# RWKV systems' stage: TensorE's order written in the program, 192 pieces of projection with the systems' steps between them

## The chip, the cores and the metric

The kernel runs on one core of a Trainium2 chip. The metric is the device time of one execution, in microseconds (us). Five engines take part, each with a queue of its own that it works off in order: TensorE (PE, matmuls), VectorE (DVE), ScalarE (ACT), GpSimd (POOL) and SyncE (SP, which issues the DMAs).

## The reference

A two-layer trunk, a gated DeltaNet layer and then an RWKV-7 layer, over 1104 tokens (16 meta tokens and 1024 of a prompt, 8 samples of 8 tokens), 1024 channels. The change is in the RWKV layer. For each of its 16 heads, with a 64x64 state `S`:

```python
rkvz = jnp.einsum('sbtd,sde->sbte', xs[:4], w_rkvz)          # four projections, 1024 x 1024 each
r, k, v, z = rkvz[0], rkvz[1], rkvz[2], rkvz[3]
kk = l2norm((k * k_k).reshape(B, T, H, N))
...
def step(S, inp):
    r_t, k_t, v_t, d_t, kk_t, b_t = inp                      # b = kk * a
    S = (S * d_t[:, :, None, :]
         + jnp.einsum('bhvk,bhk->bhv', S, -kk_t)[..., None] * b_t[:, :, None, :]
         + v_t[..., None] * k_t[:, :, None, :])
    return S, jnp.einsum('bhvk,bhk->bhv', S, r_t)
```

The kernel doesn't step token by token. It cuts time into chunks of 64 tokens; in a chunk the steps are a lower triangular 64x64 system for each head, built from `kk`, `a` and the decays, and the inverse of that system is all that the later walk over the chunks needs.

## The kernel before

The program has three parts: the DeltaNet layer (to about 1300 us), a stage in which the RWKV layer's projections and systems are made (the subject here), and a wave that walks over the chunks and ends with the output projection.

**Projections.** Each of r, v and z (`m` = 0, 2, 3) is 8 output tiles of 128 channels, over three segments of the tokens (384, 384, 336 columns; z has the first two here). One tile and segment is 24 matmuls into one PSUM buffer `d`: 8 slices of the inputs (`xa`, `xc`, `xh`, `xl`), each as high times high, low times high and high times low of a float32 split in two parts (`whi`, `wlo` of the weights). `project` (L1152) loads a tile's weights, runs its segments and has ACT copy (or gate) the result to `ev` and SP store it. Ahead of each `m`, `mix` (L1017) makes the inputs: per slice and segment two instructions on ACT, one or two on DVE into `mixs`, and a low part on DVE or POOL.

**Systems.** There are 24 items (8 pairs of heads, 3 segments), an item has 6 chunks. `rwkv_inverse` (L1293) takes a group of five items, in these steps:

- preparation: loads of the cumulated decays, `a` and `k` (`sldcs`, `slda`, `sldk`); ACT scales `k` to `skk` and takes two exponentials (`sDp`, `siD`) and a square (`sgl`); DVE makes `sal` (L1285) and, after POOL's product with `a` (L1310), the final `skk` (L1311); both are stored for the wave
- the item's system: 12 products of 64x64 on PE into PSUM `fL`, and the sums of squares by one matmul with the two-column mask `hmask` into PSUM `frss`; ACT copies `fL` to `sgl`, DVE copies `frss` to `rkc` (L1327), and SP stores both to DRAM (`rltd`, `rssd`). `fL` and `frss` share two PSUM buffers
- of the group, read back from DRAM: scales (`bblk`, and `rk` by a transpose `fbpp`), then 120 blocks of 32x32 at once in `invA`; DVE scales `invA` (L470) and inverts all blocks by 31 pairs of a product `invtmp` and a subtraction in `invT` (L452, L454). `invT` has one buffer: POOL clears it (L446, L447) once the previous group's inverse is stored
- the merge of each item (`inverse_merge`, L506): 12 products `mY` of 32x32 on PE, scaled by DVE to `invY` (L518), and 12 products `mU` with `sTT`, which ACT negates into `sTT`; POOL scales it (L1336) and SP stores it to DRAM `ttd`. `sTT` has three buffers for the five items of a group, which POOL clears (L484) and DMAs fill from the stored inverse.

**What sets the order.** The program calls `rwkv_inverse` after output tiles 1, 4, 7, 10 and 13 of the 24, with a group's five items and five merges at one place. A scheduler then orders each engine's queue when the program is built, from its own estimates of time: an instruction that it thinks ready may go ahead of others of the program. The order on the chip is fixed from then on. Only the wave's PE order is the program's own (`manual_schedule` in `layer1`).

## Time and profile before

| | us |
|---|---|
| median of three runs | 2360.84 (2356.81 to 2362.48) |
| the profiled execution's own time | 2362.64 |
| its span, first to last instruction | 2360.9 |
| PE busy | 2167.1 (92%) |
| DVE busy | 1571.2 (67%) |
| ACT busy | 1282.6 (54%) |
| POOL busy | 949.4 (40%) |

The stage runs from the first matmul of r at 1460.1 us to the first of the wave's (`zz`) at 1861.0 us of the span. A row of the profile names the line, the engine, the operation, and the tile written and those read; busy time of PE counts matmuls that overlap only once, so a stretch is read by starts. "Idle before" is the idle time of the engine just ahead of an instruction, with what ended it.

### The profile page before, as it was taken

To read this page: it belongs to the slowest core of one execution; us is meant where nothing else is said; L and a number is where in the kernel's file an instruction comes from. 1 tells how busy PE (TensorE), PEld (TensorE's weight loads), DVE (VectorE), ACT (ScalarE), POOL (GpSimd) and SP (SyncE) were. 2 spreads that over 40 slices of the span, in tenths; PEclk is the share of its full clock that TensorE was granted. 3 is DMA by queue.
4 is the path that set the end of the run, shared out by engine and by line. 5 is a ranking of instruction groups with operands and counts; after the bars stand their busy time and mean duration, and the time that the engine had idled before them with its cause. 6 is when DMAs were issued, how large, how long until landed. Compare 5 with 4: busy or idle time off the path is not lost. (4 is left out here: it accounts for less than half of the span.)

```text
span 2360.9 us, 54503 instructions
## 1 busy us (share of the span) xinstructions
PE 2167.1 (92%) x19737; PEld 1961.9 (83%) x19737; DVE 1571.2 (67%) x4219; ACT 1282.6 (54%) x3599; POOL 949.4 (40%) x1318
## 2 busy tenths in 40 slices
PE   6989999999999999999999999999888888899886
PEld 5888989889898989898989998887777866778775
DVE  6878677685858686774345833479878456667754
ACT  5455545564656555456333746646444355677763
POOL 3445333443435353434232523446445423344433
PEclk9999999999999999999999999998999998999998
DMA  3423332323233333335152145577774654677753
GB/s 113 107 76 104 88 94 78 101 75 105 78 101 91 90 102 88 109 90 184 48 163 83 52 163 175 182 199 197 188 181 130 178 160 143 178 220 227 215 153 126
DMA packets 499719, 308.89 MB, mean 131 GB/s; under 512 B 208089, under 2 KB 484826, under 8 KB 499450
## 3 DMA queue, kind: packets, MB, share of 16 engines
q1 hardware_dynamic: 499450, 305.41, 45.6%
q8 instruction: 156, 2.56, 0.5%
q14 instruction: 113, 0.93, 0.1%
HBM read 209.97 MB, written 95.33 MB: 129 GB/s over the span
## 5 line engine op out<-in xcount | busy, mean ns | idle before, releaser
L90 POOL TENSOR_TENSOR wlo<-wraw,whi 128x512 fp32r<-128x512 f32 (+2 forms) x252 | 332.4, 1322 | 359.8 <-ACT whi L86 334.4
L76 PE MATMUL d<-xc,whi 128*128 128x384 f32 (+2 forms) x910 | 260.2, 344 | 8.1 <-ACT whi L86 3.6
L86 ACT CAST whi<-wraw 128x512 fp32r<-128x512 f32 (+2 forms) x252 | 151.7, 603 | 138.8 <-PE dq L76 50.7
L419 DVE SCALAR_TENSOR_TENSOR cvy<-raw,cw,cvy 128x408 f32<-128x408 f32 (+2 forms) x288 | 178.3, 632 | 15.7 <-ACT cvy L62 13.8
L452 DVE TENSOR_TENSOR invtmp<-invA,invT 72x31 f32<-72x31 f32 (+31 forms) x403 | 172.7, 429 | 18.7 <-POOL invT L447 8.0
L76 PEld LDWEIGHTS d<-xc,whi 128*128 128x128 f32 (+1 forms) x910 | 168.9, 193 | 15.2 <-ACT whi L86 4.7
L454 DVE TENSOR_TENSOR invT<-invT,invtmp 72x31 f32<-72x31 f32 (+31 forms) x403 | 172.3, 428 | 6.6
L76 PE MATMUL dz<-xc,whi 128*128 128x384 f32 (+1 forms) x480 | 149.4, 343 | 0.0
L76 PE MATMUL dv<-xc,whi 128*128 128x384 f32 (+1 forms) x480 | 146.8, 335 | 0.0
L76 PE MATMUL d<-xa,whi 128*128 128x384 f32 (+3 forms) x450 | 141.4, 348 | 4.1 <-DVE xa L90 2.8
L76 PE MATMUL d<-xc,wlo 128*128 128x384 f32 (+2 forms) x428 | 143.9, 345 | 0.7 <-POOL wlo L90 0.7
L868 POOL TENSOR_SCALAR Sb<-Sb,eglb 128x128 f32<-128x128 f32 x128 | 80.4, 645 | 87.6 <-DMA Sb<-in_state_gdn 36.6
L76 PE MATMUL dz<-xa,whi 128*128 128x384 f32 (+1 forms) x288 | 100.3, 348 | 0.0
L76 PE MATMUL dv<-xa,whi 128*128 128x384 f32 (+1 forms) x288 | 99.9, 347 | 0.1
L76 PEld LDWEIGHTS d<-xa,whi 128*128 128x128 f32 (+1 forms) x450 | 85.2, 194 | 12.8 <-issue 5.2
L76 PEld LDWEIGHTS dz<-xc,whi 128*128 128x128 f32 x480 | 89.5, 192 | 0.8
L76 PEld LDWEIGHTS dv<-xc,whi 128*128 128x128 f32 x480 | 88.6, 188 | 0.5 <-issue 0.4
L76 PE MATMUL d<-xa,wlo 128*128 128x384 f32 (+3 forms) x252 | 86.6, 344 | 0.0
L62 ACT ACTIVATE o<-rA,gcol 128x128 f32<-128x128 f32 x128 | 46.6, 372 | 72.6 <-DVE S L779 72.0
L76 PE MATMUL d<-xh,wlo 128*128 128x384 f32 (+1 forms) x256 | 83.9, 343 | 2.0 <-POOL wlo L90 2.0
L76 PEld LDWEIGHTS d<-xc,wlo 128*128 128x128 f32 (+1 forms) x428 | 82.1, 194 | 4.0 <-issue 1.9
L76 PE MATMUL d<-xh,whi 128*128 128x384 f32 (+1 forms) x256 | 84.5, 344 | 0.5 <-ACT whi L86 0.5
(509 smaller groups left out, 7012.3 us busy)
## 6 DMA issues: line engine op xcount, KB each, us to landing
wraw<-in_gdn_w_in SPq DMA_DIRECT2D x96, 256.0 KB
wraw<-in_rwkv_w_rkvz SPq DMA_DIRECT2D x80, 256.0 KB
Sb<-in_state_gdn SPq DMA_DIRECT2D x64, 256.0 KB
wraw<-in_rwkv_w_o SPq DMA_DIRECT2D x40, 256.0 KB
E<-drow SPq DMA_DIRECT2D x24, 384.0 KB
attn<-drow SPq DMA_DIRECT2D x24, 384.0 KB
wraw<-in_gdn_w_out SPq DMA_DIRECT2D x36, 256.0 KB
out_s_gdn<-Sb SPq DMA_DIRECT2D x32, 256.0 KB
```

The source lines that it names most:

```text
L62: return self.nc.scalar.activation(out, in_, func, bias=bias, scale=scale, **kw)
L76: self.nc.tensor.matmul(out, lhsT, rhs, start=start, stop=stop)
L86: nc.scalar.copy(hi, x)
L90: e.tensor_tensor(lo, x, hi.bitcast(F32), op=ALU.subtract)
L419: nc.vector.scalar_tensor_tensor(y[:, 0:wd], raw[:, k:k + wd], cw[k], y[:, 0:wd], op0=ALU.mult, op1=ALU.add)
L452: nc.vector.tensor_tensor(tmp, A[:, j, j + 1:32].unsqueeze(2).broadcast_to([nb, n, m]), Tv[:, j, 0:m].unsqueeze(1).broadcast_to([nb, n, m] ...
L454: nc.vector.tensor_tensor(Tv[:, j + 1:32, 0:m], Tv[:, j + 1:32, 0:m], tmp, op=ALU.subtract)
L868: nc.gpsimd.tensor_scalar(Sb[:, u], Sb[:, u], self.eglb[:, hv, 4 * g + u:4 * g + u + 1], None, op0=ALU.mult)
```

## The change

`project` becomes a generator, `project_units`, that stops after each eight matmuls: 16 tiles of nine units and 8 of six, 192 in all. `rwkv_inverse` becomes `inverse_plan`, a table from the number of a unit to the steps that follow it; the whole runs under `manual_schedule` for PE, so that PE's order is the program's. The other engines' queues are still the scheduler's. An item's system (`lower`) stands after unit 9, 12, 15, 18, 21 for the first five items and every four units after that, its preparation (`prepare`) 5 or 7 units earlier. The group's inverse is called two units after its last item. The merge is split into a left half (`mY`, `merge_left`) and a right half (`mU`, `merge_right`), which stand two units apart, three units from item to item, from 35 units after the first group's last item and 27 units after the end of the group before (or later).

Buffers: `sal` and `bk` (before `skk`) are two halves of a tile with two buffers, the squares have a buffer of their own (`ssq`), and `skk` is now `k`'s own load. The loads of decays, `a` and `k` are one DMA (`cak`), `r` and `v` in the wave one (`rv`), the stores of `sal` and `bk` one (`abd`). The mask has 32 columns, and the sums of squares are three matmuls of 128 columns into three quarters of the partitions, copied by DVE as 96x128 and stored by three DMAs. One memset of each item on POOL is gone.

```diff
...
+    def dense_units(self, w, xh, xl, seg):
+        c0, n = SEGS[seg]
+        p = self.ps("d", 4)
+        his, los = w
+        for c in range(24):
+            k, j = divmod(c, 3)
+            wh, wl = his[k // 4][:, k % 4], los[k // 4][:, k % 4]
+            l, r = ((wh, xh[k]), (wl, xh[k]), (wh, xl[k]))[j]
+            self.mm(p[:, 0:n], l, r[:, c0:c0 + n], start=c == 0, stop=c == 23)
+            if c in (7, 15):
+                yield
+        yield p
...
+    def project_units(self, m, k, x, dst, apart=False):
         nc, t = self.nc, self.t
         w = self.load_w(self.i["rwkv_w_rkvz"][0, m][:, 128 * k:128 * k + 128])
-        ps = (self.dense(w, 128, *x, s, bufs=4) for s in range(2 if m == 3 else 3)) if apart else self.dense3(w, 128, *x)
-        for (c0, n), p in zip(SEGS, ps):
+        ps = None if apart else self.dense3(w, 128, *x)
+        for s, (c0, n) in enumerate(SEGS[0:2] if m == 3 else SEGS):
+            if apart:
+                for p in self.dense_units(w, *x, s):
+                    if p is None:
+                        yield
+            else:
+                p = ps[s]
             f = t(self.ev, [128, 384], "ev", 3)
             if m == 3:
                 self.gate(f[:, 0:n], p[:, 0:n])
             else:
                 nc.scalar.copy(f[:, 0:n], p[:, 0:n])
             nc.sync.dma_start(dst[k][:, c0:c0 + n], f[:, 0:n])
+            yield
...
+            self.hmask = t(ap, [128, 32], "hmask")
+            nc.gpsimd.memset(self.hmask, 0.0)
+            for h in (0, 1):
+                nc.gpsimd.memset(self.hmask[64 * h:64 * h + 64, h:h + 1], 1.0)
...
+    def inverse_plan(self, pool):
         nc, t = self.nc, self.t
-        ltd, ssd = self.dram([nth, 128, 64], f"rltd{b}"), self.dram([nth, 128], f"rssd{b}")
-        for q, n in enumerate(items):
+        plan = {}
+        G = [Ctx() for _ in range(5)]
+        keep = {}
+        def at(u, f, *x):
+            plan.setdefault(u, []).append((f, x))
+        def prepare(n):
             s, p = divmod(n, 8)
-            names = ("cs", "a", "k")
+            names = ("cak",)
             ld = self.ahead or self.rwkv_load(n, pool, "s", names)
-            kk, Dp, iD = self.rwkv_keys(p, ld, pool, "s")
+            kk, ab = ld["k"], t(pool, [128, 2, 384], "sal", 2)
+            al, bk = ab[:, 0].rearrange("p (c k) -> p c k", k=64), ab[:, 1]
+            self.act(kk, kk, AF.Identity, scale=self.pcol["rwkv_k_k"][:, p:p + 1])
+            self.act(ab[:, 0, 1:384], ld["c"][:, 0:383], AF.Exp, scale=-self.DEC)
+            self.act(bk, ld["c"], AF.Exp, scale=self.DEC)
             self.ahead = self.rwkv_load(n + 1, pool, "s", names) if n < 23 else None
-            sq = t(pool, [128, 384], "sgl", 2)
+            sq = t(pool, [128, 384], "ssq", 1)
             self.act(sq, kk, AF.Square)
-            al = t(pool, [128, 6, 64], "sal", 1)
-            self.alpha(al, kk, Dp, s, nc.vector)
+            nc.vector.tensor_tensor(ab[:, 0, 1:384], kk[:, 1:384], ab[:, 0, 1:384], op=ALU.mult)
+            nc.gpsimd.tensor_copy(al[:, :, 0:1], kk.rearrange("p (c k) -> p c k", k=64)[:, :, 0:1])
+            if s == 0:
+                nc.gpsimd.tensor_copy(al[:, 0, :].rearrange("p (b r) -> p b r", r=8)[:, :, 0:1],
+                                      kk[:, 0:64].rearrange("p (b r) -> p b r", r=8)[:, :, 0:1])
             nc.gpsimd.tensor_tensor(kk, kk, ld["a"], op=ALU.mult)
-            nc.vector.tensor_tensor(kk, kk, iD, op=ALU.mult)
-            nc.sync.dma_start(self.ald[n], al.rearrange("p c k -> p (c k)"))
-            nc.sync.dma_start(self.bkd[n], kk)
+            nc.vector.tensor_tensor(bk, kk, bk, op=ALU.mult)
+            nc.sync.dma_start(self.abd[n], ab.rearrange("p x k -> p (x k)"))
+            keep[n] = sq, bk, al
+        def lower(b, q):
+            n, g = 5 * b + q, G[b]
+            s, p = divmod(n, 8)
+            sq, bk, al = keep.pop(n)
+            ltd, ssd = g.ltd, g.ssd
             gp = self.ps("f", 2, "L")
             ssp = self.ps("f", 2, "rss")
             for c in range(6):
                 for h in (0, 1):
                     a = 64 * h
-                    self.mm(gp[a:a + 64, 64 * c:64 * c + 64], kk[a:a + 64, 64 * c:64 * c + 64], al[a:a + 64, c, :])
-            self.mm(ssp[0:2, 0:384], self.hmask, sq)
+                    self.mm(gp[a:a + 64, 64 * c:64 * c + 64], bk[a:a + 64, 64 * c:64 * c + 64], al[a:a + 64, c, :])
+            for g in range(3):
+                self.mm(ssp[32 * g:32 * g + 32, 0:128], self.hmask, sq[:, 128 * g:128 * g + 128])
             gl = t(pool, [128, 6, 64], "sgl", 2)
             nc.scalar.copy(gl, gp[:, 0:384].rearrange("p (c i) -> p c i", i=64))
             if s == 0:
                 nc.gpsimd.tensor_tensor(gl[:, 0, :], gl[:, 0, :], self.m_strs2, op=ALU.mult)
             nc.sync.dma_start(ltd[6 * q:6 * q + 6].rearrange("c q i -> q c i"), gl)
-            kc = t(pool, [2, 384], "rkc", 1)
-            nc.vector.tensor_copy(kc, ssp[0:2, 0:384])
-            nc.sync.dma_start(ssd[6 * q:6 * q + 6].rearrange("c (h i) -> h c i", h=2), kc.rearrange("h (c i) -> h c i", c=6))
-        rk2 = self.rk2[:, 30 * b:30 * b + nth]
-        blk = self.block_scale(ssd, rk2, pool)
-        TT = [t(pool, [128, 6, 64], "sTT", 3) for _ in items]
-        T1n, L21 = t(pool, [128, 30, 32], "T1n", 1), t(pool, [128, 30, 32], "L21", 1)
-        self.inverse_blocks(f"r{b}", ltd, blk, pool, TT, T1n[:, 0:nth], L21[:, 0:nth], nth)
-        for q, n in enumerate(items):
-            self.inverse_merge(L21, TT[q], T1n, rk2[:, 6 * q:6 * q + 6], pool, 6 * q, 6)
-            nc.gpsimd.tensor_tensor(TT[q], TT[q], rk2[:, 6 * q:6 * q + 6].unsqueeze(2).broadcast_to([128, 6, 64]), op=ALU.mult)
-            nc.sync.dma_start(self.ttd[n], TT[q].rearrange("p c k -> p (c k)"))
+            kc = t(pool, [96, 128], "rkc", 1)
+            nc.vector.tensor_copy(kc, ssp[0:96, 0:128])
+            for g in range(3):
+                nc.sync.dma_start(ssd[6 * q + 2 * g:6 * q + 2 * g + 2].rearrange("c (h i) -> h c i", h=2),
+                                  kc[32 * g:32 * g + 2].rearrange("h (c i) -> h c i", c=2))
+        def scale(b):
+            g = G[b]
+            blk = self.block_scale(g.ssd, g.nth, pool)
+            g.TT = [t(pool, [128, 6, 64], "sTT", 3) for _ in range(g.nth // 6)]
+            g.T1n, g.L21 = t(pool, [128, 30, 32], "T1n", 1), t(pool, [128, 30, 32], "L21", 1)
+            self.inverse_blocks(f"r{b}", g.ltd, blk, pool, g.TT, g.T1n[:, 0:g.nth], g.L21[:, 0:g.nth], g.nth)
+        def columns(b):
+            g = G[b]
+            self.column_scale(g.ssd, self.rk2[:, 30 * b:30 * b + g.nth], pool)
+        def left(b, q):
+            g = G[b]
+            n = 5 * b + q
+            g.m = m = {} if q == 0 else g.m
+            m[q] = self.merge_left(g.L21, g.T1n, self.rk2[:, 6 * n:6 * n + 6], pool, 6 * q, 6)
+        def right(b, q):
+            g = G[b]
+            n, T = 5 * b + q, g.TT[q]
+            self.merge_right(g.m.pop(q), T, 6)
+            nc.gpsimd.tensor_tensor(T, T, self.rk2[:, 6 * n:6 * n + 6].unsqueeze(2).broadcast_to([128, 6, 64]), op=ALU.mult)
+            nc.sync.dma_start(self.ttd[n], T.rearrange("p c k -> p (c k)"))
+        end = 0
+        for b, g in enumerate(G):
+            g.nth = 6 * min(5, 24 - 5 * b)
+            g.ltd, g.ssd = self.dram([g.nth, 128, 64], f"rltd{b}"), self.dram([g.nth, 128], f"rssd{b}")
+            for q in range(g.nth // 6):
+                n = 5 * b + q
+                u = 9 + 3 * n if n < 5 else 21 + 4 * (n - 4)
+                at(max(u - (5 if n < 5 else 7), 0), prepare, n)
+                at(u, lower, b, q)
+            at(u + 2, scale, b)
+            at(u + 12, columns, b)
+            end = max(end, u + 6) + 27
+            for q in range(g.nth // 6):
+                at(end + 2 + 3 * q, left, b, q)
+                at(end + 4 + 3 * q, right, b, q)
+        return plan
...
-        for n, (m, k) in enumerate(todo):
-            if k == 0:
-                x = self.mix(m, xb, slots[m], SEGS[0:2] if m == 3 else SEGS)
-            self.project(m, k, x, {0: self.rd, 2: self.vd, 3: self.zd}[m], k in range(8))
-            if n in (1, 4, 7, 10, 13):
-                self.rwkv_inverse((1, 4, 7, 10, 13).index(n), ip)
-            if n == 16:
-                zin = self.gate_inputs(xa, xb)
+        plan = self.inverse_plan(ip)
+        def units(x):
+            for n, (m, k) in enumerate(todo):
+                if k == 0:
+                    x = self.mix(m, xb, slots[m], SEGS[0:2] if m == 3 else SEGS)
+                yield from self.project_units(m, k, x, {0: self.rd, 2: self.vd, 3: self.zd}[m], True)
+        with tc.manual_schedule(engines={mybir.EngineType.PE}):
+            for u, _ in enumerate(units(x)):
+                for f, a in plan.pop(u, ()):
+                    f(*a)
+                if u == 9 * 16 + 6:
+                    zin = self.gate_inputs(xa, xb)
+        assert not plan
```

On PE, in the ninth output tile, where the first group's merges stand (`d` is a projection's PSUM buffer, the numbers behind names tell buffers apart), the order before was:

```order
L76 MATMUL d_20856<-xa_112,whi_20846 128x384
L76 MATMUL d_20856<-xa_112,wlo_20847 128x384
L76 MATMUL mU_18899<-sTT_18737,invY_18896 32x32
L76 MATMUL d_20856<-xa_112,whi_20846 128x384
L76 MATMUL d_20856<-xa_112,whi_20852 128x384
L76 MATMUL d_20856<-xa_112,wlo_20853 128x384
L76 MATMUL mU_18899<-sTT_18737,invY_18896 32x32 x11
L76 MATMUL mY_18916<-T1n_18742,L_3313_18743 32x32 x12
L76 MATMUL frss_20194<-sgl_20184,hmask_84 2x384
L76 MATMUL d_20856<-xa_112,whi_20852 128x384 x2
L76 MATMUL d_20856<-xa_112,wlo_20853 128x384
L76 MATMUL d_20856<-xa_112,whi_20852 128x384
```

and now, at the place where the second group's first right half stands, during the tenth output tile:

```order
L76 MATMUL d_20956<-xa_104,whi_20713 128x384
L76 MATMUL d_20956<-xa_104,wlo_20714 128x384
L76 MATMUL d_20956<-xa_104,whi_20713 128x384
L76 MATMUL d_20956<-xa_104,whi_20719 128x384
L76 MATMUL d_20956<-xa_104,wlo_20720 128x384
L76 MATMUL d_20956<-xa_104,whi_20719 128x384 x2
L76 MATMUL mU_20973<-sTT_19364,invY_20802 32x32 x12
L76 MATMUL fL_20990<-sal_20679 64x64 x12
L76 MATMUL frss_20991<-ssq_20685,hmask_18157 32x128 x3
L76 MATMUL d_20956<-xa_104,wlo_20720 128x384
L76 MATMUL d_20956<-xa_104,whi_20719 128x384
L76 MATMUL d_20956<-xh_2812_15534,whi_20719 128x384
```

Before, one item's `mU` and the next item's `mY` stood together, an item's sums `frss` beside them, and the projection's matmuls were split around them at any place. Now a half stands behind a unit's eighth matmul, its other half two units on, and the sums are three matmuls of 32x128.

On DVE, between the second group's inverse and its merges, the order before was (`invtmp` and `invT` are the inverse of the second group, `mixs`, `xl` and `xa` the mixing of v's inputs, `skk`, `sal` and `rkc` an item's preparation and sums, `invY` a merge of the first group):

```order
L90 TENSOR_TENSOR xa_112<-mixs_20824,xa_112 128x336
L454 TENSOR_TENSOR invT_19583<-invT_19583,invtmp_19598 120x27x5
L1311 TENSOR_TENSOR skk_20257<-skk_20257,siD_20260 128x384
L452 TENSOR_TENSOR invtmp_19601<-invA_19579,invT_19583 120x156
L1078 SCALAR_TENSOR_TENSOR mixs_20834<-xb_2714_14525,pcol_386,mixs_20834 128x336
L518 TENSOR_TENSOR invY_18995<-mY_18982,rk_10_97 32x192 x2
L454 TENSOR_TENSOR invT_19583<-invT_19583,invtmp_19601 120x26x6
L1078 SCALAR_TENSOR_TENSOR mixs_20839<-xb_2715_14526,pcol_386,mixs_20839 128x336
L452 TENSOR_TENSOR invtmp_19604<-invA_19579,invT_19583 120x175
L90 TENSOR_TENSOR xl_2814_15543<-mixs_20834,xh_2813_15542 128x336
```

and now the first `invY` of the second group stands behind the third group's inverse and the mixing of z's inputs:

```order
L1367 COPY rkc_20752<-frss_20733 96x128
L448 TENSOR_TENSOR invtmp_20063<-invA_20026,invT_20030 120x231
L1080 SCALAR_TENSOR_TENSOR mixs_22292<-xb_2711_14515,pcol_378,mixs_22292 128x64
L450 TENSOR_TENSOR invT_20030<-invT_20030,invtmp_20063 120x21x11
L1083 SCALAR_TENSOR_TENSOR mixs_22292<-xb_2711_14515,pcol_378,mixs_22292 128x320
L448 TENSOR_TENSOR invtmp_20066<-invA_20026,invT_20030 120x240
L450 TENSOR_TENSOR invT_20030<-invT_20030,invtmp_20066 120x20x12
L1338 TENSOR_TENSOR sal_20765<-sldcak_20683,sal_20765 128x383
L1344 TENSOR_TENSOR sal_20679<-sldcak_20608,sal_20679 128x384
L448 TENSOR_TENSOR invtmp_20069<-invA_20026,invT_20030 120x247
L1080 SCALAR_TENSOR_TENSOR mixs_22299<-xb_2712_14516,pcol_378,mixs_22299 128x64
L519 TENSOR_TENSOR invY_20802<-mY_20789,rk_9_93 32x192 x2
```

From the first group's `invA` to this `invY` DVE now has 259 instructions: 149 of the inverses, 28 of preparations (`sal`), 14 `rkc`, 12 `invY`, 43 of the mixing and 13 of scales and `invA`. Five others than inverses stand between the last `invT` of one group and the first `invtmp` of the next, for the first two groups.

76 lines of the change are left out of this document (33 added, 43 removed).

## The prediction

> **What bounds the kernel now.** I read the forty slices of the page first: TensorE (PE) is busy nine tenths of nearly every slice, and no other engine comes near, so the kernel's time is PE's work plus the time PE waits or runs at a lower clock. Then I cut out the stage that the change rebuilds, with busy time by stretch of time; a row gives start and end, length, then busy time and instructions of PE, its weight loads, DVE, ACT and POOL, then granted clock, DMA share and GB/s.
>
> ```profile
> 1460.00:1861.00 401.00, 362.99 (x3331) 321.43 (x3330) 292.29 (x592) 206.03 (x443) 193.91 (x278) 0.93 0.66 179
> 1460.00:1490.00 30.00, 23.75 (x108) 21.33 (x107) 23.56 (x35) 27.78 (x61) 17.38 (x30) 0.83 0.52 171
> 1592.70:1660.00 67.30, 60.85 (x618) 51.23 (x618) 59.69 (x126) 40.58 (x93) 39.43 (x46) 0.88 0.74 194
> 1475.50:1485.70 10.20, 8.82 (x26) 8.19 (x27) 8.51 (x13) 9.41 (x22) 5.85 (x12) 0.50 0.63 202
> ```
>
> The stage takes 401 us. PE is idle 38 us of it, and the granted clock is 0.93, which costs up to 28 us more (0.07 x 401); the last row shows such a stretch at half clock. DVE is busy 292 us, and in the third stretch nearly 60 of 67. PE's waits here, by what ended them (total us, times, longest):
>
> ```profile
> PE fL L76 <- DVE skk L1311: 9.8, 5, 4.1
> PE mU L76 <- issue: 4.7, 3, 2.9
> PE mY L76 <- DMA T1n<-r_t: 4.1, 2, 3.8
> PE d L76 <- ACT whi L86: 3.6, 2, 2.8
> PE d L76 <- POOL xc L90: 2.8, 1, 2.8
> ```
>
> Most are small steps of the systems (`fL`, `mU`, `mY`) that a static order put in front of projections (`d`) which could have run.
>
> **PE's own work after the change.** Projections first. These rows bracket, by the timeline, 31 matmuls of 384 columns and 23 of 336 (a row's x also counts those that reach over its ends):
>
> ```profile
> 1855.58:1861.01 5.43, 5.43 (x32) 5.43 (x32) 3.94 (x4) 2.73 (x6) 3.48 (x20) 1.00 0.98 284
> 1861.01:1864.54 3.53, 3.53 (x25) 3.53 (x24) 2.64 (x4) 1.77 (x4) 1.96 (x2) 1.00 0.98 324
> ```
>
> So a matmul takes 0.175 us and 0.153 us. The stage has 1152 of the first and 384 of the second: 201.0 + 58.8 = 259.8 us. A unit of eight is 1.396 or 1.224 us. What a step between them costs is read from PE's timeline (start, duration):
>
> ```profile
> 1523.55 0.34 PE L76 MATMUL d<-xh,wlo 128*128 128x384 f32 x1
> 1523.82 0.92 PE L76 MATMUL fL<-sal,skk 64*64 64x64 f32 x24
> 1524.67 0.81 PE L76 MATMUL frss<-sgl,hmask 128*2 128x384 f32 x2
> 1525.40 0.45 PE L76 MATMUL d<-xl,whi 128*128 128x384 f32 x1
> 1525.69 0.34 PE L76 MATMUL d<-xh,whi 128*128 128x384 f32 x1
> ...
> 1849.62 0.51 PE L76 MATMUL d<-xc,whi 128*128 128x384 f32 x2
> 1850.06 0.57 PE L76 MATMUL mU<-sTT,invY 32*32 32x32 f32 x24
> 1850.55 0.44 PE L76 MATMUL d<-xc,wlo 128*128 128x384 f32 x1
> 1850.83 0.34 PE L76 MATMUL d<-xc,whi 128*128 128x384 f32 x1
> ```
>
> One item's products `fL` stand 0.85 us, its sums `frss` 0.73, and the change of shape costs 0.1 on either side, 1.8 us in all. `frss` becomes three matmuls of 128 columns that write different quarters of the partitions. No row shows that shape. If they follow each other it stays 0.73 us, if all three run side by side it is a third, 0.24. The nearest row is `fL`, whose halves lie in different quarters of the array: 24 x 64 columns in 0.85 us are 0.55 ns a column, against 0.95 for `frss` (2 x 384 in 0.73). I take that ratio: 0.42 us, so 1.48 us an item, 35.5 us for 24, with 31 to 43 as ends. [...]
>
> A merge half alone (`mU` above) costs 0.69 us with its edges. Before, a right half and the next left half mostly went out together; now all 48 stand alone: 33.1 us. Five transposes of scales at 0.3 make 1.5. Sum: 259.8 + 35.5 + 33.1 + 1.5 = **329.9 us**, against 401 now. The saving is in waits and clock, not in work.
>
> **What stays or takes their place.** The start is untouched: the first projections need the mixed inputs, and mixing ends late.
>
> ```profile
> 1460.11 0.33 PE L76 MATMUL d<-xa,whi 128*128 128x384 f32 x1
> ...
> 1475.73 0.69 PE L76 MATMUL d<-xc,whi 128*128 128x384 f32 x1 [2.80 <-POOL xc L90]
> ...
> 1479.57 0.65 PE L76 MATMUL d<-xa,whi 128*128 128x336 f32 x1 [1.16 <-ACT xa L86]
> ...
> 1487.92 0.94 POOL L90 TENSOR_TENSOR xl<-mixs,xh 128x336 fp32r<-128x336 f32 x1 [1.28 <-ACT xh L86]
> ```
>
> The last piece of the third segment is there at 1488.9. The old order ran the second output tile meanwhile; the new one holds PE on the first until then, so its nine units end at about 1489.6, 29.5 us after the start (12.0 of them work).
>
> From there units 9 to 21 and five items: 10 x 1.396 + 3 x 1.224 + 5 x 1.48 = 25.0 us, so the fifth item's system is out at 54.5 us. Then DVE decides. Its first inverse before:
>
> ```profile
> 1532.76 0.81 PE L76 MATMUL frss<-sgl,hmask 128*2 128x384 f32 x2
> ...
> 1545.22 1.23 DVE L470 TENSOR_TENSOR invA<-invA,bblk 120x1024 f32<-120x1024 f32 x1 [2.98 <-DMA invA<-rltd]
> ...
> 1547.94 0.31 DVE L452 TENSOR_TENSOR invtmp<-invA,invT 120x31 f32<-120x31 f32 x1
> ...
> 1582.06 0.18 DVE L454 TENSOR_TENSOR invT<-invT,invtmp 120x31 f32<-120x31 f32 x1
> ...
> 1585.65 0.96 POOL L446 MEMSET invT<- 120x1024 f32 x1 [1.27 <-ACT xa L86]
> ...
> 1587.72 0.15 POOL L447 MEMSET invT<- 120x32 f32 x1
> L1327 DVE COPY rkc<-frss 2x384 f32<-2x384 f32 x24 | 13.1, 544 | 1.0 <-PE frss L76 0.2
> 1545.20:1582.20 37.00, 35.29 (x77) 1.00 0.70 209
> 1602.40:1662.10 59.70, 55.91 (x119) 0.94 0.75 199
> ```
>
> The last item's sums end at 1533.5, and `invA` starts 11.7 us later, by way of DRAM. The last two rows are DVE alone: 91.2 us for 196 instructions, 0.465 each. In DVE's new order 259 instructions stand from the first `invA` to the second group's first `invY` (149 of the inverses, 28 of the items' preparation, 14 `rkc`, 12 `invY`, 43 of the next projection's mixing, 13 small): 120 us. `rkc` shrinks from 2x384 to 96x128; a copy of that shape stands nowhere, so between nothing and the present 0.54 us; half of it takes off 4. Added are 2.7 us before the first product, and twice 3.3 us between inverses: `invT` has one buffer and is ready 5.6 us after the last product, and five other instructions (2.3 us) stand in that gap. So `invY` is done 11.7 + 116 + 9.3 = 137 us after the fifth item, at 191.5.
>
> PE reaches the right half that needs it after units 22 to 85 (43 + 21), 15 items, 11 halves and three transposes: 85.7 + 22.2 + 7.6 + 0.9 = 116.4 us, at 170.9. **It waits about 21 us** there, or in parts just before, where the items' PSUM buffers need `rkc` and the third segment of the next projection needs its mixing from the same DVE queue. What stands behind on PE is every remaining projection. The inverse's 149 instructions are the price of that wait: at the 0.18 us of the last product quoted they would be 42 us cheaper and the wait gone; at the 0.54 us of `rkc`, dearer by 11. I keep 0.465, from two whole inverses.
>
> After it: units 86 to 191 (85 + 21) 144.4 us, four items 5.9, 37 halves 25.5, two transposes 0.6: 176.4 us. DVE then has slack: 247 instructions to the last group's first `invY` and two gaps are 115 + 7 = 122 us, against 137 of PE's work to the same place. I add 10 us: 5 for weights and mixing, as in the waits quoted, and 5 for half clock, half of one stretch of 10.2 us. [...]
>
> Sum: 29.5 + 25.0 + 137 + 176.4 + 10 = **378 us** against 401 (1460.1 to 1861.0: 400.9).
>
> **What lies beside other work.** Two buffers for `sal`/`bk` and a buffer of its own for the squares take `skk` off PE's waits (9.8 us, in the sums above as no wait). Three loads become one, two stores one, one tiny store three: SP issues fewer, and PE waits on none of these; if that cover were gone, a load ahead costs what the 11.7 us path shows at most. The wave behind the stage has the same matmuls; its inputs come in two loads for five, a step pair ahead. I cost it at nothing, with 4 us either way.
>
> **Rivals.** (A) PE is the bound and the DVE wait does not come: 378 - 21 = 357, without the added 10 it is 347. For it: DVE is idle 109 us in the stage now. Against: 60 of 67 in its dense part. Profiled time 2308 to 2319. (B) Every step stands fixed before the projections behind it, and what DVE and ACT miss by is paid each time: at 0.3 us, over 72 steps, 22 us; the gain is eaten and the time stays within 0.3%, which is about what a measurement of this kernel can tell from no change. (C) Slower, by the ring of three `sTT` buffers:
>
> ```profile
> POOL sTT L484 <- DMA ttd<-sTT: 25.0, 11, 5.6
> L1336 POOL TENSOR_TENSOR sTT<-sTT,rk 128x384 f32<-128x384 f32 x24 | 23.3, 969 | 22.3 <-ACT sTT L62 19.9 <-DMA ald<-sal 1.4 <-POOL sTT L484 0.3
> ```
>
> An item's right half needs the buffer that the third item before it has scaled, stored and freed. PE allows nine units, up to two items and five halves, some 17 us; scale, store, clearing and refill are 1 + 5.6 + 0.5 + about 2 us without queues. Nine items stand so. If the queues of ACT, POOL and SP make it 20.5 us, 9 x 3.5 = 31 us go, and the kernel is 8 us slower; above that it decides. Each engine's queue moved, so it can't be excluded; POOL is idle half the stage, which speaks against it. That the order isn't fixed as said is no rival: it stands in the program.
>
> **How the numbers follow.** The profiled run took 2362.6 us, its span 2360.9; the median of three is 2360.8. 401 - 378 = 23, so the profiled time becomes 2340 and the median 2338. Forecast 0.53 (2326 to 2352), A 0.22 (2306 to 2326), B 0.12, C 0.13. Faster by over 0.3% (below 2353.8) is the forecast and A, 0.75; the same 0.13; slower 0.12. The range leaves out the lowest of A and most of C: 2308 to 2362. The unknown costs (`frss` 7 us, the wave 4, the inverses 11 up) lie in it.
>
> **What would show it.** The stage 378 us long; one lasting wait of PE near 170 to 190 us into it, ended by DVE (`invY`, `rkc` or mixing), no `skk` among its waits; `frss` near 0.42 us; 48 merge halves alone; later waits on weights only. Wrong if PE's idle time in the stage is under 25 us (A), or if most of it stands before `mU` and ends on `sTT` (C).

## The result and the profile after

The changed kernel takes 2375.02 us (median of 8 runs, 2372.42 to 2384.32), the kernel before 2361.95 us (8 runs, 2356.43 to 2372.91). The ratio is 1.0052, 95% interval 1.003 to 1.0073: slower by half a per cent, where 2338 us had been forecast. The profiled execution took 2372.42 us, 9.8 us more than that of before; its span is 2370.3 us, 9.4 us more. The stage before the change ran from 1460.1 to 1861.0 us; it now runs from 1458.2 to 1873.8 us. So the stage is 14.7 us longer, began 1.9 us earlier, and the wave behind it is 3.4 us shorter.

These are stretches of the profile after, with the columns of the first fence of the prediction: the whole stage, its start, the start of the second projection (v), and the end.

```profile
1458.20:1873.80 415.60, 363.34 (x3428) 327.12 (x3427) 286.03 (x598) 207.43 (x447) 191.03 (x261) 0.92 0.66 179
1458.20:1490.20 32.00, 21.73 (x87) 17.55 (x86) 23.05 (x37) 28.64 (x63) 20.81 (x34) 0.83 0.47 155
1634.00:1663.00 29.00, 20.90 (x126) 17.02 (x127) 26.43 (x59) 22.07 (x48) 16.51 (x21) 0.72 0.66 172
1812.00:1873.80 61.80, 61.65 (x513) 59.03 (x512) 20.09 (x38) 22.70 (x48) 28.51 (x51) 1.00 0.65 193
```

PE is busy as long as before (363), idle 52 us instead of 38, and the granted clock is 0.92 instead of 0.93. The last row shows what the program wanted everywhere: the last 62 us of the stage at full clock, almost without a wait. The row above it shows the worst place: 29 us with 8 us idle and a clock of 0.72.

PE's waits in the stage, by what ended them (total us, times, longest):

```profile
PE fL L76 <- DVE sal L1344: 6.7, 5, 2.4
PE d L76 <- DVE xa L90: 4.4, 2, 2.8
PE mU L76 <- issue: 4.3, 2, 2.4
PE d L76 <- ACT xa L86: 4.2, 3, 2.9
PE frss L76 <- DVE rk L487: 4.0, 3, 2.3
PE d L76 <- ACT whi L86: 3.5, 1, 3.5
PE fbpp L73 <- DMA invR<-rssd: 2.9, 1, 2.9
PE mY L76 <- DMA T1n<-r_t: 2.7, 2, 2.5
PE mU L76 <- DVE invY L519: 2.6, 4, 1.1
PE mU L76 <- ACT ssq L62: 1.9, 1, 1.9
...
```

The wait of 20 us that was forecast is not there: there are 37, of 0.2 to 3.5 us, at every kind of step. The rows of `mU` that name an ACT instruction or "issue" are waits for DVE too: in all six of these waits, `mU` starts 0.1 us behind the end of DVE's first `invY` instruction. The timeline of one of them, PE first, then DVE, just before the second right half of the first group:

```profile
1598.73 1.19 PE L76 MATMUL mU<-sTT,invY 32*32 32x32 f32 x24 [2.37 <-issue]
```

```profile
1595.97 0.29 DVE L1367 COPY rkc<-frss 96x128 f32<-96x128 f32 x1 [3.77 <-DMA rssd<-rkc]
...
1598.28 0.74 DVE L519 TENSOR_TENSOR invY<-mY,rk 32x192 f32<-32x192 f32 x2
```

PE stands at `mU` until `invY` is written. DVE had stood 3.8 us at `rkc` ahead of it: `rkc` has one buffer, written last at 1582.5, and its stores to DRAM, three of them now, were issued by SP only from 1593.0 on. So an instruction that nobody hurries for holds up the one that PE needs. DVE waits for others in turn, here in the whole stage:

```profile
DVE invY L519 <- PE mY L76: 25.0, 9, 4.2
DVE sal L1338 <- ACT sal L62: 18.6, 9, 3.8
...
DVE sal L1344 <- POOL sldcak L1343: 10.6, 5, 3.8
```

The waits of `sal` for ACT and POOL all lie before 1672, where the inverses are dense. Of the waits for PE, 17.1 us lie after 1800, when the last inverse is done, and hold up nothing that PE needs soon; the other 8.0 us lie between 1672 and 1750.

### The profile page after: what moved, and what is told of

It reads as the page before. It is cut to its first block, busy times and chain, and to the rows that moved or that the text cites. A ratio compares the mean times of both kernels' runs of the same rounds, so it can differ in the third digit from the quotient of the medians.

```text
span 2370.3 us, 54468 instructions
## 1 busy us (share of the span) xinstructions
PE 2162.4 (91%) x19833; PEld 1960.0 (83%) x19833; DVE 1562.2 (66%) x4219; ACT 1280.9 (54%) x3599; POOL 943.5 (40%) x1294
## 5 line engine op out<-in xcount | busy, mean ns | idle before, releaser
L448 DVE TENSOR_TENSOR invtmp<-invA,invT 72x31 f32<-72x31 f32 (+31 forms) x403 | 173.0, 429 | 20.9 <-POOL invT L443 9.5
L76 PE MATMUL d<-xl,whi 128*128 128x384 f32 (+1 forms) x256 | 84.7, 347 | 2.6 <-POOL xl L90 2.1
```

The lines of the kernel that those rows point to most:

```text
L76: self.nc.tensor.matmul(out, lhsT, rhs, start=start, stop=stop)
L448: nc.vector.tensor_tensor(tmp, A[:, j, j + 1:32].unsqueeze(2).broadcast_to([nb, n, m]), Tv[:, j, 0:m].unsqueeze(1).broadcast_to([nb, n, m] ...
```

## The experiments

Three theories stood at first. **Theory 1**: PE's written order stops in front of single steps that come a little late, and each stop brings half clock behind it. **Theory 2**: DVE has too much to do in the stage, whoever orders PE. **Theory 3**: another edit costs the time (buffers, sums, loads, the split merges). **Theory 4** was added after the first runs: the other engines' queues together set the pace, so a wait removed at one kind of step comes back at another.

Ratios are to the kernel before, timed on the same chip; the medians of before there were 2360 to 2366 us. Stage, idle time of PE in it and time at half clock while PE ran (from the records of clock) are from each profile:

| run | median us | ratio (95%) | stage | idle | half clock |
|---|---|---|---|---|---|
| before | 2361.95 | 1 | 400.9 | 38.0 | 50.5 |
| after | 2375.02 | 1.0052 (1.003 to 1.0073) | 415.6 | 52.3 | 57.5 |
| pe_by_scheduler | 2366.89 | 1.0006 (0.9993 to 1.0019) | 401.2 | 46.7 | 49.9 |
| right_late | 2373.84 | 1.0037 (1.0024 to 1.0049) | 410.8 | 48.7 | 55.0 |
| half_inverse | 2379.36 | 1.0059 (1.0037 to 1.0081) | 411.7 | 52.5 | 47.8 |
| weights_first | 2375.81 | 1.0046 (1.003 to 1.0062) | 415.2 | 52.4 | 55.4 |
| free_inputs | 2372.48 | 1.0034 (1.0012 to 1.0057) | 410.1 | 46.4 | 56.7 |
| more_distance | 2370.51 | 1.0033 (1.0013 to 1.0053) | 402.3 | 41.9 | 50.4 |
| bk_pool | 2368.85 | 1.003 (1.0013 to 1.0047) | 406.1 | 47.7 | 47.7 |
| sched_and_pool | 2376.91 | 1.0057 (1.0032 to 1.0083) | 414.3 | 49.0 | 75.8 |
| zero_fill | 2382.74 | 1.0097 (1.0079 to 1.0115) | 416.5 | 40.9 | 34.8 |
| paired_halves | 2373.97 | 1.0074 (1.0057 to 1.0091) | 405.3 | 50.8 | 44.7 |
| v_no_mix | 2360.18 | 0.9992 (0.9974 to 1.0011) | 398.4 | 39.6 | 47.5 |
| free_at_v | 2366.59 | 1.0004 (0.9989 to 1.0019) | 408.2 | 48.1 | 51.5 |
| distance_free_v | 2368.26 | 1.0016 (1.0 to 1.0033) | 407.6 | 43.7 | 54.5 |

Single executions of one kernel differ by some 10 us here, so the ratio decides, and a profile shows where the waits stand, not how large a difference is. The profiles of weights_first and zero_fill are of an execution at the end of its range: 17 us above the median of weights_first, and 9 us below that of zero_fill.

### The written order taken away

```diff
-        with tc.manual_schedule(engines={mybir.EngineType.PE}):
+        if True:
             for u, _ in enumerate(units(x)):
```

> The changed kernel with one edit undone: in the stage the scheduler orders PE again (the split of the merges, the plan of units, the buffers, the sums and the merged loads stay). Theory 1 (fixed order: PE stands in front of steps that DVE, ACT and POOL deliver 1 to 3 us late, and each wait brings half clock behind it): PE's idle time in the stage falls from 52 us to under 40, and the time from 2375 to 2345 to 2362. Theory 2 (DVE's work is the bound in the dense part, whoever orders PE): 2365 to 2378, the waits stay, on other steps. Theory 3 (another edit of the change costs the time): 2370 to 2380 with fewer waits.

The time is that of before within 0.2%: the 11 us go with the written order, and with it the other edits together cost and bring nothing (theory 3 falls). Two things are mixed in this run all the same. The scheduler also orders the other engines' queues anew: of DVE's 1728 instructions behind 1300 us some 300 stand at another place than after the change. And the equal time is a balance: against before, PE has 8 us less work and 9 us more idle time. By the ratio the time lies between theory 1's range and theory 2's. Its waits, with the scheduler's order:

```profile
PE frss L76 <- DVE rk L487: 8.4, 3, 3.7
PE fL L76 <- DVE sal L1344: 8.4, 6, 2.2
...
PE d L76 <- ACT whi L86: 2.4, 2, 1.7
```

The idle time didn't fall under 40 us as expected. The steps wait no less than in the written order; what is shorter are the waits of the projections, before `d`: 7.6 us in all (the sum over PE's gaps), against 20.2 with the written order. PE's own work is also 5 us smaller, 329.5 us at full clock against 334.6 (busy time less half of the time at half clock; an estimate from the spacing of matmuls of 384 columns, which in the stage before follow each other by 0.175 us at full clock and 0.32 at half, by the medians). One likely cause is seen in its timeline, where a right half and a left half go out together, a few of their matmuls mixed:

```profile
1608.26 0.47 PE L76 MATMUL mU<-sTT,invY 32*32 32x32 f32 x17
...
1608.63 0.48 PE L76 MATMUL mY<-T1n,L 32*32 32x32 f32 x19
1609.04 0.44 PE L76 MATMUL d<-xc,whi 128*128 128x384 f32 x1
```

46 of the 48 matmul records of two halves take 0.78 us here, from the first start to the next `d`. Two halves alone are 0.98 us by the same reckoning (2 x 0.49), and have four changes of shape of 0.1 us at their edges instead of two. So a pair saves up to 0.4 us; how many pairs make up the 5 us was not counted.

### Distance, and half of DVE's inverse

```diff
-                at(end + 4 + 3 * q, right, b, q)
+                at(end + 7 + 3 * q, right, b, q)
```

> The changed kernel with every right half of a merge three units later (five units of 1.4 us behind its left half instead of two). Theory 1 (too little distance between a step and what DVE must do for it): the waits of PE before mU fall from 14.0 us to under 4, half clock shrinks by 10 to 20 us of running time, and the time falls by 12 to 20 us to 2355 to 2363. Theory 2 (DVE is full): the waits come back before other steps and the time stays within 5 us, 2370 to 2380.

```diff
-        for j in range(31):
+        for j in range(0, 31, 1 if nb == 72 else 2):
```

> The changed kernel without every second pair of product and subtraction of the stage's inverses on DVE (15 of 31 pairs left out in each of the five groups, some 85 us of DVE). Theory 2 (DVE's amount of work is the bound): the waits that end on DVE (fL 7.6, frss 4.0, mU 14.0, part of d's 20.2 us) go almost whole and the time falls by 35 to 45 us to 2330 to 2340. Theory 1 (distance and order, not amount): the waits fall by a third to a half, since the instruction that PE waits for still stands behind others that wait for ACT and POOL; 2350 to 2365.

Both expectations of theory 1 fail in the time; right_late lies in theory 2's range. The waits moved as they should: with the right halves later, those before `mU` went from 14.0 us to none, and these stand in their place.

```profile
PE frss L76 <- DVE rk L487: 10.4, 4, 4.7
PE fL L76 <- DVE sal L1344: 8.5, 6, 2.5
```

Theory 2 fails with the second run. Its DVE is busy 227 us of the stage instead of 286, yet PE is idle as long as before. The waits that end on DVE did shrink, but one of 11.5 us is new:

```profile
PE fbpp L73 <- DMA invR<-rssd: 14.2, 3, 11.5
```

`invR` is the load for a transpose of scales. SP issued the stores that it reads at 1568, and the load itself at 1588, with 28 other issues between. With the shorter inverse the scheduler had built another order, SP's included: 12 of the 28 issues are loads of `sTT` that stand behind the load of `invR` after the change. So this one wait may hide a part of what the shorter inverse brings, but its 11.5 us are far from the 35 to 45 us that theory 2 forecast. Hence theory 4.

### Every input of a step free

```diff
+        C = self.C = t(pool, [128, 448], "const", 1)
...
-                    self.mm(gp[a:a + 64, 64 * c:64 * c + 64], bk[a:a + 64, 64 * c:64 * c + 64], al[a:a + 64, c, :])
+                    self.mm(gp[a:a + 64, 64 * c:64 * c + 64], Z[a:a + 64], Z[a:a + 64])
```

(and so for `frss`, `fbpp`, `mY` and `mU`; `Z` is a part of `C`)

> The changed kernel, but PE's steps of the systems (fL, frss, fbpp, mY, mU) read a constant tile in place of bk, sal, ssq, invR, T1n, L21, invY and sTT, so that PE waits for no input of a step; all other engines do all their work, and PE's order and number of matmuls are the same. Theory 1 (the time is in waits for steps' inputs and the half clock behind them): idle time of PE in the stage falls from 52 to under 28 us (the start 10 and the mixing of v 10 stay), half-clock running from 57 to under 30 us, and the time to 2325 to 2340. Rival (PE's own work is longer than counted, by the stops between units and the changes of shape): over 2360.

Theory 1 in its first form falls here: PE waits for no input of a step, and the time hardly changes.

```profile
PE frss L76 <- DVE rk L487: 13.6, 4, 6.0
PE d L76 <- POOL wlo L90: 7.1, 7, 1.9
PE mU L76 <- ACT sTT L62: 5.5, 3, 2.9
...
PE fL L76 <- ACT sgl L1366: 3.4, 1, 3.4
```

The steps now wait for their results' readers. `frss` shares two PSUM buffers with `fL` and `fbpp`; `fbpp` holds one until DVE comes to `rk`, and so on for `mU` behind ACT's copy. PE is tied to the others at both ends of a step, by its inputs and by the buffer of its result. The rival, more work on PE, falls too: its work is 335.4 us.

### Remedies one by one and together

The weights of v's and z's first tiles ahead of the mixing; `bk`'s product on POOL; more distance at all steps with the transposes in the merges' PSUM buffers; all of it with the halves in pairs:

```diff
+                    if m:
+                        w = self.load_w(self.i["rwkv_w_rkvz"][0, m][:, 0:128])
                     x = self.mix(m, xb, slots[m], SEGS[0:2] if m == 3 else SEGS)
...
-            nc.vector.tensor_tensor(bk, kk, bk, op=ALU.mult)
+            nc.gpsimd.tensor_tensor(bk, kk, bk, op=ALU.mult)
...
-        ps = self.ps("f", 2, "bpp")
+        ps = self.ps("m", 2, "bpp")
...
-            at(u + 12, columns, b)
+            at(u + 16, columns, b)
...
-                at(end + 2 + 3 * q, left, b, q)
-                at(end + 4 + 3 * q, right, b, q)
+                at(end + 4 + 3 * q, left, b, q)
+                at(end + 9 + 3 * q, right, b, q)
```

> The changed kernel with the weights of the first tile of v and of z loaded and split before the mixing of their inputs in the program, so that ACT's and POOL's splits do not stand behind the mixing. Theory 1: of the 10.6 us of waits at the start of v the first two (ACT whi 3.5, POOL wlo 1.2) go, and half of that comes back in the waits for the mixing behind them; 2370 to 2373. If the mixing alone sets the start of v: no change, 2374 to 2377.

> The changed kernel with one instruction of each item moved: the product that makes bk on POOL instead of DVE, PE's order the same. Theory 1: the waits before fL fall from 7.6 us to under 3 and the time by 4 to 8 us, 2366 to 2371. Theory 4: the waits turn up elsewhere, within 3 us of the changed kernel, 2372 to 2378.

> The changed kernel with more distance at every kind of step: left halves two and right halves five units later (right three units further behind left), the transposes of scales four units later and in the merges' PSUM buffers, and the product that makes bk on POOL instead of DVE. Theory 1 (waits belong to single steps that stand too close behind their inputs): the 31 us of waits before fL, frss, fbpp, mY and mU fall under 10, half clock with them, 2345 to 2358. Theory 4 (the waits are conserved: what PE doesn't lose at one step it loses at the next, because the other engines' queues together set the pace of the first two thirds): idle time stays over 42 us, 2366 to 2378.

> All remedies for the fixed order together: more distance at left and right halves (as in the run with more distance), transposes four units later in the merges' PSUM buffers, bk's product on POOL, the weights of the first tiles of v and z ahead of the mixing, and each right half right ahead of the left half of the second item after it, so that 14 pairs of halves stand together on PE. Against the run with more distance (2370.5): pairs save 0.2 to 0.3 us each, 3 to 4 us; weights 0 to 3 us. Theory 1: 2362 to 2367, still not faster than before by more than 0.3%. Theory 4 (waits are conserved): 2367 to 2374.

(In the last, right halves stand at `end + 10 + 3 * q`.)

Weights first: no change. `bk` on POOL and more distance: each about 5 us less than the change (ratios 1.003 and 1.0033 against 1.0052; the intervals overlap, so the gain isn't certain). In the run with more distance the waits before steps fell from 31 to 14 us and those before `d` rose from 20 to 27, most of what is left:

```profile
PE d L76 <- POOL wlo L90: 9.6, 7, 2.5
PE fL L76 <- POOL sal L1344: 6.7, 5, 2.2
```

The weights' low parts and `bk` are now both POOL's. The pairs missed: PE's work fell by 3 us as expected, but the waits before `d` went to 34 us, and the kernel is slower than with distance alone. For `bk` on POOL the time lies in theory 1's range, but not by its mechanism: the waits before `fL` rose from 7.6 to 9.1 us. No remedy of the four brought what its own waits were worth, which is what theory 4 says; its bound for more distance, idle time over 42 us, was just missed (41.9), and the pairs came out above its range when they are taken by the ratio.

```diff
-        with tc.manual_schedule(engines={mybir.EngineType.PE}):
+        if True:
...
-        ps = self.ps("f", 2, "bpp")
+        ps = self.ps("m", 2, "bpp")
...
-            nc.vector.tensor_tensor(bk, kk, bk, op=ALU.mult)
+            nc.gpsimd.tensor_tensor(bk, kk, bk, op=ALU.mult)
```

> The changed kernel with PE ordered by the scheduler in the stage, the transposes of scales in the merges' PSUM buffers and bk's product on POOL. Theory 1: the waits before fL and frss (13.7 and 8.4 us with the scheduler's order) fall by half and the time by 5 to 12 us against the run with the scheduler's order alone: 2352 to 2362. Theory 4: no gain, 2363 to 2370.

A miss on both theories: by the ratios 12 us slower than with the scheduler's order alone. The scheduler built another order from these two edits, and PE runs 76 us at half clock in it. Why this order is worse was not found. It shows by how much two orders can differ that the scheduler holds to be good, and so how much weight a single run with a new order can bear.

### The start of v

```diff
-                if k == 0:
+                if k == 0 and m != 2:
                     x = self.mix(m, xb, slots[m], SEGS[0:2] if m == 3 else SEGS)
```

> The changed kernel without the mixing of v's inputs (v is projected from r's inputs; 24 pieces of mixing, some 130 instructions on ACT, DVE and POOL, are left out), so that PE has nothing to wait for at the start of v. Theory 1: the waits there (10.6 us) and the 10 us of half clock behind them go, 2352 to 2362. Theory 4 (the other engines' queues pace PE as a whole): the gain is larger, since DVE and ACT lose some 25 to 30 us of work each, and the waits at steps fall too, under 2352. If neither (waits come back elsewhere): 2366 to 2376.

Theory 1's range holds: 14 us by the ratios (1.0052 less 0.9992) go with the mixing of v. But the run takes work from three engines besides. So the order alone was changed at that place:

```diff
+            if u in (62,):
+                order.close()
+            if u in (89,):
+                order.enter_context(tc.manual_schedule(engines={mybir.EngineType.PE}))
```

> The changed kernel with PE's order left to the scheduler in 27 units around the start of v only (units 63 to 89; 505 of PE's matmuls stand otherwise, all the others as in the changed kernel). If the loss of the fixed order is at v's start, where it has nothing to put in front of PE while v's inputs are mixed: the waits before d fall from 20.2 to under 13 us and the time comes down to that of the run with the scheduler's order throughout, 2360 to 2367. If the loss lies in the waits at single steps all over the first two thirds: 2370 to 2376.

The time is that of the scheduler's order throughout, and its interval ends below that of the change. PE's waits from 1630 us on, over the start of v, first after the change (to 1665), then with these 27 units left to the scheduler (to 1675):

```profile
PE d L76 <- ACT whi L86: 3.5, 1, 3.5
PE d L76 <- DVE xa L90: 2.8, 1, 2.8
PE d L76 <- ACT xh L86: 1.5, 1, 1.5
PE d L76 <- POOL wlo L90: 1.2, 1, 1.2
...
```

```profile
PE fL L76 <- DVE sal L1344: 4.5, 2, 3.2
PE frss L76 <- DVE rk L487: 0.3, 1, 0.3
PE mY L76 <- DMA T1n<-r_t: 0.2, 1, 0.2
```

With the three rows left out (1.4 us), 10.4 us of waits before `d` became none, and 5 us before steps. The waits before `d` in the whole stage are 18.1 us, not under 13 as expected, because a new one of 6.4 us, for weights, stands at 1732 in this profile; and those before `fL` rose to 14.0 us. What filled the gap at v's start is not steps but projection: matmuls of 384 and of 336 columns, so of different PSUM buffers, alternate, where the written order finishes one segment before it begins the next.

```profile
1653.14 0.32 PE L76 MATMUL d<-xc,whi 128*128 128x336 f32 x1
1653.29 0.33 PE L76 MATMUL d<-xl,whi 128*128 128x384 f32 x1
1653.46 0.32 PE L76 MATMUL d<-xc,wlo 128*128 128x336 f32 x1
...
1642.00:1671.00 29.00, 24.00 (x209) 21.61 (x208) 26.20 (x57) 22.46 (x49) 17.16 (x22) 0.88 0.67 176
```

In these 29 us over the start of v PE does 20.9 us of work at full clock, in the 29 us after the change that are quoted above 14.8: 6 us of the 7.4 by which this run's stage is shorter. Up to about 1600 us the queues of DVE, ACT and POOL are the same in both runs; behind it they differ too, on DVE in some 140 instructions.

> The run with more distance (2370.5) with the same 27 units left to the scheduler. If distance and the start of v are two separate losses (4.5 and 8 to 14 us): 2354 to 2363, the same as before the change or a little faster. If they are one and the same: 2363 to 2372.

The two gains don't add up: 1.0016, between its parents. The intervals of all three overlap. No version found beats the kernel before.

### Half clock

```diff
+            if c in (7, 15, 23):
+                for _ in range(self.fill.get(self.unit, 0)):
+                    self.mm(p[:, 0:n], self.zero, xh[0][:, c0:c0 + n], start=False, stop=False)
...
```

> The changed kernel with 145 matmuls of a zero weight tile (each 0.153 to 0.175 us, 25 us in all, they add nothing to the sums) put into PE's order just ahead of the steps at which PE waited longest: 4 to 12 each ahead of the first group's first left half and three of its right halves, five later steps, the first tile of v, and 5 in each of the first nine units of v. In the records so far a window of 3.41 us with over 1.7 us of idle PE was followed by a window at half clock in nearly every case, and one with under 1.2 us in almost none. If that rule is the cause: PE's idle time falls by about the zeros' 25 us, half-clock running in the stage falls from 57 to under 35 us, and the time falls by 5 to 14 us to 2361 to 2370, although PE does more. Rival (half clock comes from something else, the waits are only beside it): half-clock running stays over 50 us and the time is the same or up to 10 us longer, 2375 to 2385.

The theory came true in part: half clock fell from 57.5 to 34.8 us, idle time by 11 us, not 25. The time did not follow: the median is 8 us above that of the change, and the stage is as long as after the change even in the profiled execution, which is the fastest of the five (2373.86 us; the others take 2382.7 to 2384.6).

```profile
1462.10:1878.70 416.60, 375.70 (x3573) 343.48 (x3572) 287.57 (x598) 207.63 (x447) 188.32 (x263) 0.95 0.66 179
```

The clock is 0.95 instead of 0.92, PE's work at full clock 358 us instead of 335 (24 of zeros), and a wait of 8.2 us before `frss`, for DVE's read of `rk`, is new. So waits do bring the half clock. Filling them with work was no gain here; that the other engines decide when PE may go on fits this and is not shown by it.

## Why the prediction was wrong

The stage's sum, forecast and measured. The measured work is busy time less half of the time at half clock: from 1490.2 us on 341.6 - 48.2 / 2 = 317.5.

| | forecast | measured |
|---|---|---|
| start, to unit 9 | 29.5 | 32.0 |
| PE's work behind it, at full clock | 318 | 317.5 |
| waits behind it | 26 | 42.0 |
| half clock behind it | 5 | 24.1 |
| stage | 378 | 415.6 |

**PE's work** behind the start was right to a microsecond (318 to 317.5). Over the whole stage it is 334.6 against the sum of 329.9; the difference lies in the first 32 us, which also hold 12 matmuls of another step (`flora`) that the sum left out. The forecast of `frss` was close:

```profile
1504.65 0.42 PE L76 MATMUL frss<-ssq,hmask 128*32 128x128 f32 x6
1505.00 0.42 PE L76 MATMUL d<-xa,whi 128*128 128x336 f32 x1
```

Three sums stand 0.35 us, forecast 0.42, 0.73 before: 2.1 times less. It is 9 us of PE's work less in 24 items; that work is less by 8 us in the run with the scheduler's order too, whose time is that of before.

**The step that failed most is "5 for half clock"**: 24 were measured, a term missed by 19 us. The prediction had read up to 28 us of half clock in the stage before and then kept 5, half of one stretch of 10.2 us, its estimate for one long wait in place of many short ones. It would have been consistent to keep the 25 us of before (50.5 / 2) until a reason for less was found: the waits stayed many and short, 37 of them.

**"It waits about 21 us there"** failed next. The forecast had DVE done with the second group's first `invY` 191.5 us into the stage and PE standing at the right half behind it from 170.9 on. Both came later, and together:

```profile
1669.55 0.57 PE L76 MATMUL mY<-T1n,L 32*32 32x32 f32 x24
1671.02 0.75 DVE L519 TENSOR_TENSOR invY<-mY,rk 32x192 f32<-32x192 f32 x2
1673.05 0.57 PE L76 MATMUL mU<-sTT,invY 32*32 32x32 f32 x24
```

`invY` is done at 1671.8, 213.6 us in, and PE is at the right half at 1673.1, 214.9 us in and without a wait. DVE's way there, from `invA` to `invY`:

```profile
1532.80:1671.80 139.00, 119.38 (x259) 0.90 0.78 209
```

It is the 259 instructions of the forecast, at 0.461 us each (forecast 0.465). What was missed is DVE's own waits: 19.6 us of these 139, forecast 9.3 with the gaps between inverses. The fifth item came 4 us later than forecast, and the path by DRAM to `invA` took 15.7 us instead of 11.7. PE meanwhile lost 44 us against the sum, in small waits and half clock. So 23 us of the stage's 38 us over the forecast had been lost by this right half and the other 14 behind it. The forecast took one chain of DVE, gave it waits only around the inverses, and let PE run free ahead of it; it left out that both are stopped at each step on the way. Of the 42 us, the rows of the waits give `mU` 13.4, `d` at the start of v 10.4, `fL` 7.5 (6.7 and a smaller row), `frss` 4.0, `fbpp` 2.9 and `mY` 2.7.

**"Two buffers for `sal`/`bk` [...] take `skk` off PE's waits"** (9.8 us): they took a third off. `fL` still waits 6.7 us for the same product (`bk` now, shown as `sal`, DVE L1344). DVE itself waits before this product, 10.6 us in the stage, for POOL's product ahead of it.

**The mixing of v** was counted among "5 for weights and mixing". With the scheduler's order at this place, matmuls of other segments filled the time in which v's inputs are mixed. The written order holds PE on one segment and has little to put beside it: between units 71 and 82 (v begins at 72) stand three items and one transpose, some 5 us. PE stops for 10.4 us, and the clock is 0.72. By free_at_v, which frees PE's order in these units, and by v_no_mix, this is where the change loses against the kernel before. What can't be excluded is that the new order of the other engines, which the scheduler makes with it, has a part: sched_and_pool shows that another order can be worth 12 us.

**The rivals.** B was the right kind (small misses at every fixed step) and too small: 22 us taken, 42 and half clock measured. C had the only time that was slower, and did not happen: no wait before `mU` ended on an `sTT` buffer. A's condition, PE idle under 25 us, was far off. **The wave** cost nothing, as forecast: 3.4 us less in one profile, and 1.4 us more in the run with the scheduler's order, which has the merged loads too.

## What to carry to other kernels

An order written for the busiest engine removes its freedom to run something else when one of its inputs is late; before it is written, find the places where that freedom is used now (here the start of a projection whose inputs are still being mixed) and put work there by hand (here the next segment's matmuls, which no run tried). Where every step ties the engine to other queues at both ends, by its inputs and by its result's buffer, waits removed at one step can come back at another, so add up the waits of all kinds, not those of the step that was mended. And price a wait with the clock that it costs: here 42 us of waits brought 24 us more.

## What the runs showed of the hardware

The records of the granted clock change on a grid of 3.413 us: in the profiles of before and after all 128 of them start on it, within 4 ns. PE's idle time in each such window, counted in fifteen profiles from 1300 to 1880 us: after a window at full clock with under 1.25 us idle, the next was at half clock in 2 cases of 2019; with 1.25 to 1.75 us in 41 of 79; with over 1.75 us in 152 of 156. At half clock, the next window stays so after 0.75 us idle or more in 72 of 72 cases, and after under 0.25 us in 8 of 195. In these counts the idle time within a window goes with half clock, and the length of a wait alone does not tell. Two pairs of neighbouring windows after the change:

```profile
1595.33:1598.74 3.41, 1.04 (x8) 0.79 (x7) 2.64 (x8) 0.00 (x0) 0.00 (x0) 1.00 0.74 185
1598.74:1602.15 3.41, 3.34 (x55) 2.64 (x56) 2.29 (x6) 2.62 (x6) 0.32 (x2) 0.50 1.13 368
1557.79:1561.20 3.41, 1.76 (x11) 1.44 (x9) 1.27 (x4) 1.73 (x4) 0.00 (x0) 1.00 0.30 70
1561.20:1564.61 3.41, 2.61 (x38) 2.37 (x39) 3.36 (x4) 2.02 (x5) 3.34 (x4) 1.00 0.97 208
```

A wait of 2.37 us within one window was followed by half clock in the next two; the second of the two is one of the 8 cases of 195, since PE is idle for under 0.1 us in the first. A wait of 2.45 us, 1.65 in one window and 0.8 in the next, cost none. The row of 10.2 us at half clock that the prediction named shows the same: it is itself busy for 8.82 us, and the window ahead of it is idle for 2.5 of 3.41 us. By these counts a wait of some 2 us that falls into one window costs an estimated 1.7 us beside itself (half of 3.41), and several such waits pay it several times. The eight waits of over 4 us in the profiles of before and after (4.1 to 5.9 us) were each followed by 2.9 to 5.8 us at half clock, the wait of 2.37 us above by 6.83. So one long wait cost no more clock here than a short one; what was wrong in the prediction is that it counted on the one long wait.
